# Weight splits of the SSD groups scheduled at the highest priority on ScalarE and VectorE

## The chip, the cores and the metric

The kernel runs on one core of a Trainium2 chip. The engines are TensorE (PE, matmuls and transposes), VectorE (DVE), ScalarE (ACT), GpSimd (POOL) and SyncE (SP), which mostly issues DMAs; each takes its own list of instructions and waits on semaphores where it needs another's result. The metric is the device time of one execution in microseconds (us).

## The reference, cut to what matters

A trunk of two layers for 512 tokens of width 1024, all in float32. Layer 0 mixes the tokens by a short gated convolution, layer 1 by a Mamba-2 SSD mixer with 8 groups; a SwiGLU network follows each. The change is in the SSD mixer:

```python
z, xbc, dt_raw = jnp.split(h @ w_in, [M_D_INNER, M_D_INNER + M_CONV_DIM], axis=-1)
xbc = jax.nn.silu(causal_depthwise_conv(xbc, conv_w) + conv_b)
xs, bm, cm = jnp.split(xbc, [M_D_INNER, M_D_INNER + g * n], axis=-1)
...
cb = jnp.einsum('bclgn,bcsgn->bclsg', cm, bm)
y_diag = jnp.einsum('bclsgr,bcsgrp->bclgrp', cb[..., None] * decay, xdt)
states = jnp.einsum('bclgn,bclgr,bclgrp->bcgrpn', bm, decay_to_end, xdt)
...
y_off = jnp.einsum('bclgn,bcgrpn,bclgr->bclgrp', cm, prev, jnp.exp(cs).astype(dtype))
...
y = y.reshape(bsz, s, M_D_INNER) * jax.nn.silu(z)
y = rms_normalize(y.reshape(bsz, s, g, M_D_INNER // g)).reshape(bsz, s, M_D_INNER) * norm_g
return y @ w_out
```

Each group has 256 columns of x, 128 of B, 128 of C and 256 of z.

## The kernel before, in words

Every float32 product is computed as three matmuls. A factor is split into a high half, rounded to the format that TensorE takes, and a low half, the rest: ACT casts the high half (L202) and DVE subtracts it from the source to get the low one (L203). The three matmuls per slice of 128 rows are high by high (L259), high by low (L260) and low by high (L261); the third is the first to need the weights' low half.

Weights come in by `load_w`: one DMA of 1 MB into a staging tile (`wst`, 2 buffers), then per 128 columns one split into a tile `whl` (4 buffers). Such a tile is the weight of one chunk: 8 slices by 3 matmuls, 24 matmuls of 512 columns into one PSUM tile `ip`. With 4 buffers the cast of a tile has to wait until PE has finished the chunk whose tile had the buffer before it, four tiles back.

A group takes six chunks: two of x (wx), B and C (wbc), two of z (wz). A pass of the loop over the groups (g = 1 to 7) finishes group g and projects group g + 1 beside it. PE's order in a pass is written by hand and fixed: wx0, `step_a` (transposes xtok and btokp, then cb), wx1, the states (`st`), wbc0, wbc1, `step_cc` (yo and yd, twice), z0, z1, and `step_d` (ssg, the norm's sum over the group). ssg needs accg, the sum of two squares of the gated output; cb needs ct and a free PSUM tile; the last matmuls of the states (L1053, st2) need the second half of xw.

The lists of ACT and DVE within the passes are made by a scheduler from priorities, which by default follow the order of the code, and from its own estimates of when operands are ready. On DVE stand, besides the splits, three taps of a convolution per chunk (cu, L957), xw and xdt from the transposed x (L1023, L1025), the mask of cb (L1037), the decay matrix csb (subtractions L1067, then a product L1074), the gated output (L1097 to L1107) and the norm (L1117, L1120). Instructions are taken in the order of the list. csb is filled by a DMA that ACT's queue issues (L944). Groups 0 and 1 lie in a stretch whose ACT and DVE order is written by hand too, with the splits passed through `later`.

Of the kernel before, what the change touches and what calls it, by code (L numbers as in the profile page):

```python
# [19 lines left out]
KD = D // P  # L20
DFF = 2816
NF = DFF // P
DIN = 2048
# [12 lines left out]
def trunk_kernel(  # L36
# [164 lines left out]
    def split_w(src, dst, nk):  # L201
        act.copy(dst[:, 0, :nk, :], src)  # L202
        dve.tensor_tensor(dst[:, 1, :nk, :], src, dst[:, 0, :nk, :].bitcast(F32), SUB)  # L203

    def load_w(srcs, nk=KD, k0=0, later=None):


        st = wst_p.tile([P, 8, 256], F32, tag="wst", name="wst")
        o = 0
        for m, c0, n in srcs:  # L210
            dma(st[:, :nk, o:o + n], m[k0 * P:(k0 + nk) * P, c0:c0 + n].rearrange("(k p) f -> p k f", p=P))
            o += n
        res = []
        for b in range(o // P):
            w = whl_p.tile([P, 2, 8, P], F32R, tag="whl", name="whl")
            sw = st[:, :nk, b * P:(b + 1) * P]
            if later is None:
                split_w(sw, w, nk)
            else:
                later.append((lambda sw=sw, w=w: act.copy(w[:, 0, :nk, :], sw),  # L220
                              lambda sw=sw, w=w: dve.tensor_tensor(w[:, 1, :nk, :], sw,
                                                                   w[:, 0, :nk, :].bitcast(F32), SUB)))
            res.append(w)
        return res
# [317 lines left out]
    wm_in, wm_out = m_w_in[0], m_w_out[0]  # L542

    with ExitStack() as ph:
# [96 lines left out]
        with tc.manual_schedule(engines={PE_ENGINE, mybir.EngineType.SP, mybir.EngineType.Activation,  # L641
# [122 lines left out]
            for name in OPENING.split():  # L764
                step(name)
            later = []
            next_cv = [load_w([(w_in0, (i + 1) * D + 2 * P, 256)], later=later) for i in range(2)]
            for hi, lo in later:
                hi()
# [20 lines left out]
        for jp in range(0, KD, 2):  # L790
            if jp == 0:
                pss = lead_ps[:4]
            else:
                ws = next_cv[0] + next_cv[1] if jp == 2 else [
                    w for i in range(2) for w in load_w([(w_in0, (i + 1) * D + jp * P, 256)])]
                pss = [in_chunk(w, h) for w in ws]
            us = [conv_mix_cv(jp + b, pss[b], pss[2 + b]) for b in range(2)]
            wb = load_w([(w_in0, jp * P, 256)]) if jp else None
            for b in range(2):
                a = act_tile(f"bu{jp + b}")  # L800
                conv_mix_b(us[b], in_chunk(wb[b], h) if jp else lead_ps[4 + b], a)
                acts.append(a)
            ada_next(2 if jp < 6 else 0)
            if jp == 4:
                put_gates(0)
                gg = make_gg(0, gg_tile)
                other_vectors(actp.tile([P, 8, P], F32, tag="a", name="rows2"))
# [57 lines left out]
    with ExitStack() as ph:  # L865
# [99 lines left out]
        class Group:  # L965
# [8 lines left out]
            def weights(self, i, later=None):  # L974
                g = self.g
                if i == 0:
                    self.wx = load_w([(wm_in, DIN + g * 256, 256)], later=later)
                elif i == 1:
                    self.wbc = load_w([(wm_in, 2 * DIN + g * P, P), (wm_in, 2 * DIN + D + g * P, P)],
                                      later=later)  # L980
                else:
                    self.wz = load_w([(wm_in, g * 256, 256)], later=later)

            def conv(self, i, pst):
                g = self.g
# [161 lines left out]
        with tc.manual_schedule(engines={PE_ENGINE, mybir.EngineType.Activation, mybir.EngineType.DVE}):  # L1147
            cur, nxt = Group(0), Group(1)
            later = []
# [365 lines left out]
```

## Time and profile before

| | |
|---|---|
| median of 3 runs | 1379.19 us (1378.7 to 1380.71) |
| profiled execution, its own time | 1379.55 us |
| its span, first to last instruction | 1377.5 us |
| PE busy | 1353.7 us, 98% |
| DVE busy | 911.7 us, 66% |
| ACT busy | 580.6 us, 42% |
| mean granted TensorE clock | 0.995 |

The passes 1 to 7 lie between some 669 and 960 us of the span; a steady pass takes 41 us. In a timeline row a number in brackets is the time for which the engine was idle ahead of the instruction, with what ended it. Matmuls are pipelined: rows of 0.39 us follow each other every 0.23 us, and a matmul that starts 0.63 us long and every 0.43 us ran at the lower granted clock.

### The profile page before, as it was taken

Reading aid. Unit: us, or ns where it says so; the run is one execution under the profiler, and the core shown is the slowest. Engines: PE = TensorE matmul, PEld = TensorE weight load, DVE = VectorE, ACT = ScalarE, POOL = GpSimd, SP = SyncE. Lnnn points to the kernel's source line nnn. Section 1 sums busy time; section 2 is a strip of 40 time slices with the busy share of each in tenths; the row PEclk is TensorE's granted clock in tenths of the full one; section 3 lists DMA queues with packets and bytes.
Section 4 is the critical chain, followed back from the end, with each engine's and each line's share of the span. In section 5 each row is a group of like instructions: output and inputs, shape, how many; then the busy total and the mean of one; then the engine's idle time right before and its main releaser. Section 6 shows DMA issues by size and latency. Waiting matters only on the chain.

```text
span 1377.5 us, 17633 instructions
## 1 busy us (share of the span) xinstructions
PE 1353.7 (98%) x6973; PEld 1135.5 (82%) x6973; DVE 911.7 (66%) x1485; ACT 580.6 (42%) x875; POOL 1.5 (0%) x11
## 2 busy tenths in 40 slices
PE   8999999999999999999899999999999999999997
PEld 7788889888888888898778888888889888887886
DVE  5777757478775222669878888777675655334867
ACT  5432247222222211665665656543473222223754
POOL 0000000000000000000000000000000000000000
PEclk9999999999999999999999999999999999999999
DMA  9956670468683322514344234332233987323743
GB/s 313 318 181 218 228 236 24 137 215 273 215 282 106 130 95 69 149 33 146 118 138 130 83 94 138 108 107 96 89 123 125 331 289 266 118 70 130 251 161 115
DMA packets 163702, 222.09 MB, mean 161 GB/s; under 512 B 7060, under 2 KB 112164, under 8 KB 161188
## 3 DMA queue, kind: packets, MB, share of 16 engines
q1 hardware_dynamic: 159616, 208.20, 45.9%
q10 hardware_dynamic: 4004, 12.77, 2.9%
q8 instruction: 55, 0.90, 0.3%
q14 instruction: 27, 0.22, 0.1%
HBM read 207.17 MB, written 13.78 MB: 160 GB/s over the span
## 4 chain that ended last, share of the span: by engine, by line
PE 64%; DVE 2%; DMA 1%; ACT 0%; issue 0%; SPq 0%; DVEq 0%; ACTq 0%
PE ip L259 11%; PE ip L261 11%; PE ip L260 11%; PE y L359 5%; PE y L361 5%; PE y L360 5%; PE li L259 2%; PE li L261 2%; PE li L260 2%; PE yd L1092 1%; PE yo L1086 1%; PE pa L1387 1%; PE pa L1388 1%; PE pz L1388 1%; PE pb L1388 1%; PE pz L1386 1%
## 5 line engine op out<-in xcount | busy, mean ns | idle before, releaser
L259 PE MATMUL ip<-h,whl 128*128 128x512 f32 x1096 | 434.2, 396 | 2.5 <-DVE cv L777 2.5
L261 PE MATMUL ip<-h,whl 128*128 128x512 f32 x1096 | 428.9, 391 | 6.6 <-DVE whl L203 6.6
L260 PE MATMUL ip<-h,whl 128*128 128x512 f32 x1096 | 427.8, 390 | 0.0
L261 PEld LDWEIGHTS ip<-h,whl 128*128 128x128 f32 x1096 | 206.4, 188 | 50.8 <-DVE whl L203 7.0
L259 PEld LDWEIGHTS ip<-h,whl 128*128 128x128 f32 x1096 | 206.7, 189 | 47.1 <-issue 5.2
L260 PEld LDWEIGHTS ip<-h,whl 128*128 128x128 f32 x1096 | 206.7, 189 | 43.2 <-issue 1.2
L202 ACT CAST whl<-wst 128x1024 fp32r<-128x1024 f32 (+1 forms) x163 | 152.2, 952 | 205.2 <-PE ip L261 161.0
L203 DVE TENSOR_TENSOR whl<-wst,whl 128x1024 fp32r<-128x1024 f32 (+1 forms) x163 | 176.9, 1101 | 61.8 <-ACT whl L202 61.1
L203 DVE TENSOR_TENSOR whlo<-wsto,whlo 128x1024 fp32r<-128x1024 f32 x46 | 56.3, 1223 | 96.6 <-ACT whlo L202 96.6
L126 DVE SCALAR_TENSOR_TENSOR ada_acc<-ada_st,csil,ada_acc 128x512 f32<-128x512 f32 x140 | 104.7, 749 | 22.8 <-DMA ada_st<-in_ada_w_dram 20.1
L202 ACT CAST whlo<-wsto 128x1024 fp32r<-128x1024 f32 x46 | 48.3, 1050 | 113.6 <-PE y L361 87.7
L259 PE MATMUL li<-h,whl 128*128 128x256 f32 x288 | 83.2, 289 | 0.0
L261 PE MATMUL li<-h,whl 128*128 128x256 f32 x288 | 81.6, 283 | 0.0
L260 PE MATMUL li<-h,whl 128*128 128x256 f32 x288 | 81.5, 283 | 0.0
L957 DVE SCALAR_TENSOR_TENSOR cu<-ip,cols,cu 128x511 f32<-128x511 f32 (+2 forms) x84 | 62.0, 741 | 13.7 <-ACT cu L954 13.5
L359 PE MATMUL y<-whlo,ff 128*128 128x512 f32 x176 | 68.6, 390 | 0.0
L361 PE MATMUL y<-whlo,ff 128*128 128x512 f32 x176 | 68.5, 389 | 0.0
L360 PE MATMUL y<-whlo,ff 128*128 128x512 f32 x176 | 68.5, 389 | 0.0
L259 PEld LDWEIGHTS li<-h,whl 128*128 128x128 f32 x288 | 55.3, 192 | 0.0
L260 PEld LDWEIGHTS li<-h,whl 128*128 128x128 f32 x288 | 55.2, 192 | 0.0
L261 PEld LDWEIGHTS li<-h,whl 128*128 128x128 f32 x288 | 55.1, 191 | 0.0
L359 PE MATMUL y<-whlo,ys 128*128 128x512 f32 x128 | 51.1, 399 | 0.0
(281 smaller groups left out, 1926.5 us busy)
## 6 DMA issues: line engine op xcount, KB each, us to landing
ada_st<-in_ada_w_dram SPq DMA_DIRECT2D x96, 512.0 KB, 5.8
wst<-in_f_w_in_dram SPq DMA_DIRECT2D x44, 1024.0 KB, 6.5
wst<-in_m_w_in_dram SPq DMA_DIRECT2D x14, 1024.0 KB, 5.7
tb<-in_f_w_out_dram SPq DMA_DIRECT2D x22, 512.0 KB, 7.4
td<-tb SPq DMA_DIRECT2D x11, 1024.0 KB, 4.9
wsto<-in_f_w_out_dram SPq DMA_DIRECT2D x10, 1024.0 KB, 4.8
wst<-in_m_w_in_dram SPq DMA_DIRECT2D x20, 512.0 KB, 5.2
wst<-in_a_w_in_dram SPq DMA_DIRECT2D x9, 1024.0 KB, 6.0
```

Source lines behind the costliest of these rows:

```text
L126: dve.scalar_tensor_tensor(acc, w, csil[:, k:k + 1], acc, MUL, ADD)
L202: act.copy(dst[:, 0, :nk, :], src)
L203: dve.tensor_tensor(dst[:, 1, :nk, :], src, dst[:, 0, :nk, :].bitcast(F32), SUB)
L259: pe.matmul(dst, w_at(w, 0, kk), a[:, 0, sl], start=start, stop=False)
L260: pe.matmul(dst, w_at(w, 0, kk), a[:, 1, sl], start=False, stop=False)
L261: pe.matmul(dst, w_at(w, 1, kk), a[:, 0, sl], start=False, stop=stop)
L359: pe.matmul(pst, a[:, 0, tk], wt[:, 0, kk, :], start=k == 0, stop=False)
L360: pe.matmul(pst, a[:, 0, tk], wt[:, 1, kk, :], start=False, stop=False)
L361: pe.matmul(pst, a[:, 1, tk], wt[:, 0, kk, :], start=False, stop=k == K - 1)
L957: dve.scalar_tensor_tensor(u[:, sft:], pst[:, :T - sft], w[3 - sft], u[:, sft:], MUL, ADD)
L1086: pe.matmul(pyo[:, sl], self.prev[:, cc - 1, q * P:(q + 1) * P], self.ct[:, sl], start=True, stop=True)
L1388: pe.matmul(acc[t], a[:, 1, sl], w[0], start=False, stop=True, skip_group_check=True)
```

## The change

`load_w` gets an argument `soon`. Where it is set, and no list `later` is given, the split's two instructions are put down under the scheduler's highest priority. The three loads of a group set it, so it acts on the splits of groups 2 to 7, and on nothing else.

```diff
-    def load_w(srcs, nk=KD, k0=0, later=None):
+    def load_w(srcs, nk=KD, k0=0, later=None, soon=False):
...
             if later is None:
-                split_w(sw, w, nk)
+                with tc.high_priority() if soon else ExitStack():
+                    split_w(sw, w, nk)
...
-                    self.wx = load_w([(wm_in, DIN + g * 256, 256)], later=later)
+                    self.wx = load_w([(wm_in, DIN + g * 256, 256)], later=later, soon=True)
...
-                                      later=later)
+                                      later=later, soon=True)
...
-                    self.wz = load_w([(wm_in, g * 256, 256)], later=later)
+                    self.wz = load_w([(wm_in, g * 256, 256)], later=later, soon=True)
```

No instruction's work changes. SP's list and POOL's are the same; on PE only the ssg of group 0 moves, from within the wx0 chunk of group 2 to its end; ACT loses two table loads and keeps all else, in another order; DVE keeps all, in another order. Lines of the new kernel past L218 are one higher.

DVE, end of pass 1's state update, before: the last cu taps of the wx1 chunk, the states' sums (prev), and behind them the splits of group 2's wbc tiles (whl_5662, whl_5665) and of its z tiles (whl_5777, whl_5780).

```order
L1056 TENSOR_TENSOR prev_5628<-prev_5628,dec_4979 128x256
L957 SCALAR_TENSOR_TENSOR cu_5622<-ip_5597,cols3_91,cu_5622 128x509
L1058 TENSOR_TENSOR prev_5628<-prev_5628,st01_5629 128x256
L1074 TENSOR_TENSOR csb_5401<-csb_5401,cbm_5590 128x1024
L1056 TENSOR_TENSOR prev_5628<-prev_5628,dec_4979 128x256
L203 TENSOR_TENSOR whl_5662<-wst_5659,whl_5662 128x1024
L1058 TENSOR_TENSOR prev_5628<-prev_5628,st2_5632 128x256
L203 TENSOR_TENSOR whl_5665<-wst_5659,whl_5665 128x1024
L203 TENSOR_TENSOR whl_5777<-wst_5775,whl_5777 128x1024
L203 TENSOR_TENSOR whl_5780<-wst_5775,whl_5780 128x1024
```

DVE in the new order, where the same two wbc splits stand now: within the gated output of group 0 (yg1) and the csb subtractions for group 2, ahead of accg and of all of pass 1's step_a.

```order
L1098 TENSOR_TENSOR y1_5441<-yo_5427,ecsb_5166 128x384
L203 TENSOR_TENSOR whl_5662<-wst_5659,whl_5662 128x1024
L1099 SCALAR_TENSOR_TENSOR yg1_5440<-xs1_4983,dcol_94,yd_5431 128x512
L1068 TENSOR_SCALAR csb_5524<-csb_5524,cs_tok_4977 128x128
L1100 TENSOR_TENSOR yg1_5440<-yg1_5440,y1_5441 128x384
L1068 TENSOR_SCALAR csb_5524<-csb_5524,cs_tok_4977 128x128
L1101 TENSOR_TENSOR yg1_5440<-yg1_5440,zs1_5207 128x512
L1068 TENSOR_SCALAR csb_5524<-csb_5524,cs_tok_4977 128x128
L203 TENSOR_TENSOR whl_5665<-wst_5659,whl_5665 128x1024
```

Both have moved up past the whole of step_a, the first states and the products of csb.

DVE at step_a of pass 1, before: the two halves of xw and xdt stand together.

```order
L1023 TENSOR_TENSOR xw_5569<-xtok_5570,dte_tok_4978 128x512
L1025 TENSOR_TENSOR xdt_5568<-xtok_5570,dt_tok_4976 128x512
L1023 TENSOR_TENSOR xw_5569<-xtok_5577,dte_tok_4978 128x256
L1025 TENSOR_TENSOR xdt_5568<-xtok_5577,dt_tok_4976 128x512
L1037 TENSOR_TENSOR cbm_5590<-cb_5591,mask_82 128x512
```

The same place in the new order, with a tap of cu and the split of group 2's first z tile in it:

```order
L1024 TENSOR_TENSOR xw_5569<-xtok_5570,dte_tok_4978 128x512
L958 SCALAR_TENSOR_TENSOR cu_5449<-ip_5373,cols3_91,cu_5449 128x509
L203 TENSOR_TENSOR whl_5777<-wst_5775,whl_5777 128x1024
L1026 TENSOR_TENSOR xdt_5568<-xtok_5570,dt_tok_4976 128x512
L1024 TENSOR_TENSOR xw_5569<-xtok_5577,dte_tok_4978 128x256
L1026 TENSOR_TENSOR xdt_5568<-xtok_5577,dt_tok_4976 128x512
```

The split and the tap have come between the first xw and the first xdt, whose source xtok holds the PSUM buffer that cb takes next.

DVE at step_a of pass 4, before: xw and xdt of group 4, then the mask and a wbc split of group 5; the split of group 5's second z tile (whl_6746) comes 13 rows below these.

```order
L1023 TENSOR_TENSOR xw_6535<-xtok_6536,dte_tok_4978 128x512
L957 SCALAR_TENSOR_TENSOR cu_6528<-ip_6503,cols3_91,cu_6528 128x509
L1025 TENSOR_TENSOR xdt_6534<-xtok_6536,dt_tok_4976 128x512
L1023 TENSOR_TENSOR xw_6535<-xtok_6543,dte_tok_4978 128x256
L1025 TENSOR_TENSOR xdt_6534<-xtok_6543,dt_tok_4976 128x512
L1037 TENSOR_TENSOR cbm_6556<-cb_6557,mask_82 128x512
L203 TENSOR_TENSOR whl_6631<-wst_6625,whl_6631 128x1024
```

The same place in the new order:

```order
L1024 TENSOR_TENSOR xw_6535<-xtok_6536,dte_tok_4978 128x512
L958 SCALAR_TENSOR_TENSOR cu_6528<-ip_6503,cols3_91,cu_6528 128x510
L1026 TENSOR_TENSOR xdt_6534<-xtok_6536,dt_tok_4976 128x512
L203 TENSOR_TENSOR whl_6746<-wst_6741,whl_6746 128x1024
L958 SCALAR_TENSOR_TENSOR cu_6528<-ip_6503,cols3_91,cu_6528 128x509
L1024 TENSOR_TENSOR xw_6535<-xtok_6543,dte_tok_4978 128x256
L1026 TENSOR_TENSOR xdt_6534<-xtok_6543,dt_tok_4976 128x512
L1038 TENSOR_TENSOR cbm_6556<-cb_6557,mask_82 128x512
```

whl_6746 now stands between the two halves of xw (xw_6535 from xtok_6536 and from xtok_6543). Its cast takes the buffer of the wx1 chunk's weights. In the other passes the split of the second z tile stands behind the second half of xw.

Likewise on DVE ahead of the ssg of pass 1: the split of group 3's first wbc tile (whl_5984) stood behind accg's sum of group 1, and now stands ahead of that sum and of the gated output's second half (y1, its sum and product); its cast takes the buffer of the first z chunk of that pass.

## Rows read from the trace of the kernel before

**Rows 1.** Page, busy time by engine (share of the span).

```profile
PE 1353.7 (98%) x6973; PEld 1135.5 (82%) x6973; DVE 911.7 (66%) x1485; ACT 580.6 (42%) x875; POOL 1.5 (0%) x11
```

**Rows 2.** What PE waited for, 640 to 1000 us: total, times, longest.

```profile
PE ip L261 <- DVE whl L203: 6.6, 1, 6.6
PE cb L1036 <- DVE xdt L1025: 0.7, 1, 0.7
```

**Rows 3.** Windows: us; PE, PEld, DVE, ACT, POOL busy (count); clock; DMA share; GB/s.

```profile
688.00:689.00 1.00, 0.00 (x0) 0.00 (x0) 1.00 (x3) 1.00 (x1) 0.00 (x0) 0.87 0.00 0
689.00:695.00 6.00, 2.83 (x7) 2.25 (x8) 6.00 (x9) 4.75 (x7) 0.00 (x0) 0.50 0.04 5
64.50:67.50 3.00, 3.00 (x7) 2.36 (x8) 3.00 (x7) 1.67 (x3) 0.00 (x0) 0.50 1.10 363
720.00:920.00 200.00, 200.00 (x1061) 165.94 (x1060) 168.37 (x271) 115.32 (x140) 0.00 (x0) 1.00 0.35 108
```

**Rows 4.** PE timeline, pass 1: start, length, instruction, [idle before <-what ended it].

```profile
677.23 1.13 PE L1036 MATMUL cb<-ct,bt 128*128 128x128 f32 x8 [0.71 <-DVE xdt L1025]
...
685.19 0.39 PE L260 MATMUL ip<-h,whl 128*128 128x512 f32 x1
692.17 0.79 PE L261 MATMUL ip<-h,whl 128*128 128x512 f32 x1 [6.60 <-DVE whl L203]
...
695.68 0.39 PE L260 MATMUL ip<-h,whl 128*128 128x512 f32 x1
```

**Rows 5.** ACT timeline, pass 1, casts of group 2's wbc tiles.

```profile
679.32 1.98 ACT L202 CAST whl<-wst 128x1024 fp32r<-128x1024 f32 x2
```

**Rows 6.** DVE timeline, pass 1.

```profile
675.80 0.69 DVE L1023 TENSOR_TENSOR xw<-xtok,dte_tok 128x512 f32<-128x512 f32 x1 [3.47 <-PE xtok L1019]
676.40 0.68 DVE L1025 TENSOR_TENSOR xdt<-xtok,dt_tok 128x512 f32<-128x512 f32 x1
...
690.90 1.22 DVE L203 TENSOR_TENSOR whl<-wst,whl 128x1024 fp32r<-128x1024 f32 x1
```

**Rows 7.** PE timeline, pass 4, end of wx1 and the states.

```profile
813.61 0.39 PE L261 MATMUL ip<-h,whl 128*128 128x512 f32 x1
...
814.29 0.39 PE L261 MATMUL ip<-h,whl 128*128 128x512 f32 x1
...
815.38 0.59 PE L1053 MATMUL st<-xw,btok 128*128 128x256 f32 x2
```

**Rows 8.** ACT timeline, pass 4, cast of the second z tile.

```profile
815.85 1.05 ACT L202 CAST whl<-wst 128x1024 fp32r<-128x1024 f32 x1
```

**Rows 9.** DVE timeline, pass 4.

```profile
812.59 0.41 DVE L1023 TENSOR_TENSOR xw<-xtok,dte_tok 128x256 f32<-128x256 f32 x1
...
815.53 0.75 DVE L957 SCALAR_TENSOR_TENSOR cu<-ip,cols,cu 128x511 f32<-128x511 f32 x1 [0.20 <-ACT cu L954]
```

**Rows 10.** DVE and PE timeline, pass 1, output of the group and ssg.

```profile
711.40 0.55 DVE L1097 TENSOR_TENSOR y<-yo,ecsb 128x384 f32<-128x384 f32 x1
...
712.81 0.28 DVE L1067 TENSOR_SCALAR csb<-csb,cs_tok 128x128 f32<-128x128 f32 x1 [0.27 <-DMA csb<-cs_d]
713.01 0.68 DVE L1100 TENSOR_TENSOR yg<-yg,zs 128x512 f32<-128x512 f32 x1
...
718.99 1.02 PE L1114 MATMUL ssg<-accg,ones 128*128 128x512 f32 x2
```

**Rows 11.** ACT's queue and DVE, pass 3; DVE and PE, pass 4.

```profile
789.70 0.33 ACTq L944 DMA_DIRECT2D csb<-cs_d  x1
...
795.33 0.29 DVE L1067 TENSOR_SCALAR csb<-csb,cs_tok 128x128 f32<-128x128 f32 x1 [0.91 <-DMA csb<-cs_d]
...
838.72 0.68 DVE L1107 TENSOR_TENSOR accg<-accg,sqg 128x512 f32<-128x512 f32 x1
...
841.40 1.02 PE L1114 MATMUL ssg<-accg,ones 128*128 128x512 f32 x2
```

**Rows 12.** PE timeline, layer 0, the end of an idle time.

```profile
64.40 0.77 PE L259 MATMUL ip<-h,whl 128*128 128x512 f32 x1 [2.55 <-DVE cv L777]
```

## The prediction

> **What bounds the kernel now.** I read the page's busy times first: PE is busy 98% of the span, DVE 66%, ACT 42% [rows 1]. So only what makes PE wait, or its clock fall, can cost or give time. Next I read the waits of PE over the passes in question (640 to 1000 us). There are two: once a matmul of L261 waits 6.6 us for a weight split on DVE (L203), once cb waits 0.7 us for an xdt [rows 2]. Both fall in pass 1. In the steady passes PE is busy for 200.00 of 200 us while DVE has 168 and ACT 115 [rows 3]: no wait is left there to take away, and every wait the new order makes there is new.
>
> Last I read the timelines around the long wait, engine by engine, to see what is behind what. On PE the second matmul of the wbc chunk starts at 685.19, the third only at 692.17 [rows 4]. ACT had cast both hi halves from 679.32 to 681.30 [rows 5]; DVE took up the first lo half at 690.90 [rows 6], 9.6 us after that cast. So the split was late by its place on DVE, not by its data. The Trainium skill ("PSUM — Partial Sum Buffer", Engine vs sequencer instructions) calls the queues of ScalarE and VectorE strict FIFO; the row agrees for this split, and by the same rule a split that is raised before its data are there holds up all behind it, which is what the added terms below are.
>
> **What goes.** In the new order the two wbc splits of group 2 stand among the group's first csb subtractions, long before their chunk. Their casts wait for the slots that the two z chunks before free. The second of these ends at about 669 (cb's 677.23 [rows 4] less 0.7 of waiting, 2 of transposes, 5.44 for the wx0 chunk of 24 matmuls and 0.45 for ssg); with a cast of 1.0 and a split of 1.2 us [rows 5, 6] both are done some 14 us before 685.2, and the wait goes whole. A steady matmul comes every 0.227 us (813.61 to 814.29 holds three [rows 7]). The third matmul was due at 685.19 + 0.23 = 685.42 and came at 692.17: 6.75. The clock had fallen meanwhile: 0.87 in 688 to 689, 0.50 (1.2 GHz) from 689 to 695 [rows 3]; the eight intervals from 692.17 to 695.68 [rows 4] took 3.51 in place of 8 x 0.227 = 1.81: 1.70 more. Together **-8.45 us**. What is late next there is nothing within 5 us.
>
> In passes 2 to 7 the edit gives nothing: four slots hold the split weights, so a cast can only begin when PE has finished the chunk four tiles back, and before it did so already (pass 4: the wx1 chunk's last matmul begins at 814.29, the cast into its slot at 815.85 [rows 7, 8], and its own chunk, z1's, is the fourth from there). The wait is hidden behind 5.4 us of matmuls per chunk. ACT has two table loads fewer; it is 42% busy and none of its table loads is waited for, so nothing.
>
> **What is added, first: cb in pass 1.** The new order puts a cu and the split of z's first tile between the first xw and the first xdt. xw starts at 675.80 and xdt 0.60 later now [rows 6]; after, the cu (0.75 [rows 9]) and the split (1.22 [rows 6]) come first, 1.97 at their lengths, about 1.8 since one instruction starts 0.08 ahead of the former's end (675.80 + 0.69 against 676.40). The split's own cast can begin when the wx0 chunk ends, four transposes (some 0.5) ahead of the xw, so it is done by 676.4, before its turn at 677.05, and adds nothing. cb already waits for that xdt (677.23 [rows 4]), so all of it shows: **+1.8** (ends 0 and 2.0), and PE's idle time there becomes 0.71 + 1.8 = 2.5 us.
>
> **Second: ssg of pass 1.** It is due when z1's chunk ends: 718.99 now [rows 10], 718.99 - 8.45 + 1.8 = 712.34 after. In the new order the split of group 3's first wbc tile stands ahead of y1, its add, its product and accg. Its cast waits for z0's chunk, 5.44 us before (707.0 with the last matmul's tail): cast to 708.1, split to 709.25, then y1, a csb subtraction (0.20, from 712.81 to 713.01), the add, another subtraction and the product: 711.40 to 713.69 now with one subtraction and 0.27 of waiting in it [rows 10], so 2.0 plus the overlap, to 711.3; five subtractions 1.0, with ACT's square beside them; accg 0.68 [rows 11] to 713.0. **+0.6** (ends 0 and +2, by whether the csb transfer has landed by then).
>
> **Third: st2 in pass 4.** Here alone z1's split stands ahead of the second xw; in the other passes it follows it. That split's cast waits for the last matmul of the wx1 chunk, and st2, five matmuls on, waits for that xw. A ring: PE's own chunk, cast, split, cu, xw, PE. From the start of the last matmul (814.29): its 0.39, cast 1.05 [rows 8], split 1.14 to 1.22, cu 0.66 to 0.75 [rows 9], xw 0.41 [rows 9], and 0.2 for the hand-overs between engines (of it 0.15 from DVE to PE: the first xdt ends at 676.40 + 0.68, cb begins at 677.23 [rows 4, 6]): 3.85 to 4.0, where st2 is due after 815.38 - 814.29 = 1.09 [rows 7]. **+2.75** (ends 2.5 and 3.1). Now the xw is done at 813.0, before that point.
>
> In the other passes the ssg has least to spare. Now accg's add ends at 839.4 and ssg starts at 841.40 [rows 11]. After, from the landing of csb: 0.2 + 0.5 + 0.2 + 0.6, seven subtractions 1.4, split 1.14, accg 0.68: 4.7 us, and ssg is due 10.9 after the transfer's issue (830.5, one chunk pair before 841.40). A landing takes 795.33 - 789.70 = 5.6 at most now [rows 11], so at least 0.6 us are left; I take nothing (ends 0 and 1 us for each of five passes).
>
> **The clock.** PE idles 2.5 us at the first place and 2.7 at the third. The nearest row: an idle time of 2.55 us ahead of 64.40 [rows 12], after which the clock stood at 0.50 from 64.5 to 67.5 [rows 3], 1.5 us lost over those 3 us at half pace. In the long wait the fall came about 3.2 us after 685.6. So one fall has been seen by 2.55 us and one only after 3.2: I give each place an even chance and **+1.7** for one fall (that of row 692.17), none or two as ends. The Trainium skill ("TensorE: Matmul & The Clock Gate", What's actually happening) says that the watch on activity runs free, so that the same gap can lower the clock in one run and not in the next; by it the three runs of the result may differ by 1.7 us, and the sum would be the same.
>
> **Sum.** -8.45 + 1.8 + 0.6 + 2.75 = -3.3, and with one fall -1.6. The profiled execution took 1379.55 (span 1377.5 and 2.05 around it), 0.36 above the median of the runs shown, 1379.19. From the median: 1375.9 with no fall, **1377.5** with one, 1379.2 with two.
>
> **Rivals.**
> Only the long wait goes (0.10): the two places where a split overtakes what PE waits for don't bite, because DVE reaches them earlier than I count. 1379.2 - 8.45 + at most 2 = 1370.7 to 1372.7. For it: in 200 us of steady passes PE never waited. Against: both places follow from the order alone, and the third is a ring with PE in it.
> No net change (0.13): both clock falls come, or the second wait is at its upper end: 1379 to 1380.5. For it, row 64.40.
> Slower (0.17): ssg is late in every pass. Place: csb's seven subtractions and the split of the next wbc tile, both ahead of accg. It decides when csb lands more than 6.2 us after its issue; splits done sooner free the staging tiles sooner, and the 1 MB weight transfers then start nearer to csb's. Price: 1 us per us beyond 6.2 in each of passes 2 to 6. At a landing of 7.5 us 1.3 x 5 = 6.5: 1377.5 + 6.5 = 1384, over 1382 from 7.1 us on. For it: csb's landing is waited for today (0.91 us of DVE at 795.33). Against: 0.6 to 1.5 us to spare as it lands now.
> The change doesn't do what it says (0.02): the split still comes late; 1379.
>
> **Chances and range.** My forecast with no or one fall has 0.58 (0.20 and 0.38), the rivals 0.10, 0.13, 0.17 and 0.02. 0.2% is 2.8 us, about what a measurement of this kernel tells from no change: below 1376.4 is faster, above 1382 slower. Faster: 0.10 + 0.17 of the case without a fall (its 1375.9 is just under the line) + 0.09 of the one-fall case, 0.36; slower 0.17; the same 0.47. The range from 1373 to 1382.5 leaves out most of the first rival and most of the slower one, 0.2 in all; the likeliest case's own range is 1375.5 to 1379.5.
>
> **What would show it.** In the new profile: no wait of L261 for L203 in the wbc chunk of pass 1; cb of pass 1 waiting about 2.5 us for xdt; the st2 of pass 4 waiting about 2.7 us for xw, with the cast just behind the chunk's last matmul; ssg of pass 1 waiting under 1 us for accg; granted clock 0.50 for some 3 us behind one of the first two. Wrong would be: any wait of PE in passes 2, 3, 5, 6 or 7; ssg waiting in pass after pass; or neither cb nor st2 waiting longer than before.

## The result, and the profile after

The changed kernel took 1388.08 us (median of 6 runs, 1384.65 to 1390.26), the kernel before 1379.88 beside it (6 runs, 1377.73 to 1381.77): ratio 1.0057, interval 1.0046 to 1.0068. It is slower by 8 us where 1.7 less was forecast. The profiled execution of it took 1384.74 us, span 1382.7, so its trace shows 5.2 of the 8 us.

The page's busy times, the answer to [rows 1], show none of it: PE is at 98% again.

```profile
PE 1355.5 (98%) x6973; PEld 1136.2 (82%) x6973; DVE 912.4 (66%) x1485; ACT 576.8 (42%) x873; POOL 1.5 (0%) x11
```

The waits of PE from 640 to 1000 us in the changed kernel (in total, times, longest), the answer to [rows 2]:

```profile
PE ssg L1115 <- DVE accg L1108: 6.4, 5, 2.3
PE st L1054 <- DVE xw L1024: 2.5, 1, 2.5
PE cb L1037 <- DVE xdt L1026: 2.5, 1, 2.5
```

The 6.6 us wait for a weight split is gone. The cb and st2 waits of the forecast are there, and ssg waits in five passes for accg. The PE timeline of the changed kernel has each of them (start, length, instruction, idle time before it):

```profile
677.23 1.45 PE L1037 MATMUL cb<-ct,bt 128*128 128x128 f32 x8 [2.50 <-DVE xdt L1026]
...
685.27 1.02 PE L1052 MATMUL st<-xw,btok 128*128 128x256 f32 x4
...
713.98 1.10 PE L1115 MATMUL ssg<-accg,ones 128*128 128x512 f32 x2 [1.67 <-DVE accg L1108]
...
756.20 1.10 PE L1115 MATMUL ssg<-accg,ones 128*128 128x512 f32 x2 [1.18 <-DVE accg L1108]
...
799.57 1.10 PE L1115 MATMUL ssg<-accg,ones 128*128 128x512 f32 x2 [2.33 <-DVE accg L1108]
...
818.70 0.70 PE L1054 MATMUL st<-xw,btok 128*128 128x256 f32 x2 [2.52 <-DVE xw L1024]
...
846.00 1.10 PE L1115 MATMUL ssg<-accg,ones 128*128 128x512 f32 x2 [0.99 <-DVE accg L1108]
...
887.29 1.10 PE L1115 MATMUL ssg<-accg,ones 128*128 128x512 f32 x2 [0.28 <-DVE accg L1108]
...
928.17 1.02 PE L1115 MATMUL ssg<-accg,ones 128*128 128x512 f32 x2
```

Against the starts before (cb 677.23 and ssg 718.99 and 841.40 in [rows 4, 10, 11]; the states of pass 1 at 683.66 and the other ssg at 759.79, 800.60, 882.21 and 923.02 in the same trace), the distance of the two kernels runs like this:

| place | after minus before, us | what lies between |
|---|---|---|
| transposes of pass 1 | -1.80 | layer 0: an idle time of 2.14, not 2.55, and no lower clock behind it |
| cb, pass 1 | 0.00 | cb waits 2.50, not 0.71 |
| states, pass 1 | +1.61 | lower clock behind that wait |
| ssg, pass 1 | -5.01 | -8.45 of the long wait, +1.67 |
| ssg, pass 2 | -3.59 | +1.18 |
| ssg, pass 3 | -1.03 | +2.33 |
| ssg, pass 4 | +4.60 | lower clock behind the wait of pass 3 (about 1.6), st2 2.52, ssg 0.99 |
| ssg, pass 5 | +5.08 | +0.28 |
| ssg, pass 6 | +5.15 | nothing |

Each ssg wait cost about 0.2 us more than its length: 1.42, 2.56 and 0.48 us from pass to pass in 2, 3 and 5, where the waits are 1.18, 2.33 and 0.28. Most of the 1.80 us of the first line (1.6) is there before 69 us of the span, in layer 0, which the change does not touch; from the transposes on, the changed kernel lost 5.15 + 1.80 = 6.95 us.

The clock, in the windows of the changed kernel (us, then busy time and count of PE, PEld, DVE, ACT, POOL, then the granted clock):

```profile
678.00:681.00 3.00, 3.00 (x10) 2.46 (x9) 2.48 (x6) 2.97 (x5) 0.00 (x0) 0.50 0.00 0
802.00:804.00 2.00, 2.00 (x6) 1.63 (x5) 0.03 (x1) 1.96 (x4) 0.00 (x0) 0.50 0.31 56
820.00:823.00 3.00, 3.00 (x15) 2.46 (x14) 3.00 (x7) 0.75 (x2) 0.00 (x0) 1.00 1.03 276
```

It was down to 0.50 (1.2 GHz) behind cb's 2.50 us of idle time, and again behind ssg's 2.33 in pass 3, and it stayed at 1.00 behind st2's 2.52.

Why ssg is late is read in pass 3, across the queues (SPq and ACTq rows are the issue of a transfer); the first row is the split of the next group's second x tile:

```profile
783.88 1.22 DVE L203 TENSOR_TENSOR whl<-wst,whl 128x1024 fp32r<-128x1024 f32 x1
...
785.12 0.37 SPq L211 DMA_DIRECT2D wst<-in_m_w_in_dram  x1
...
786.19 0.33 ACTq L945 DMA_DIRECT2D csb<-cs_d  x1
...
794.77 0.29 DVE L1068 TENSOR_SCALAR csb<-csb,cs_tok 128x128 f32<-128x128 f32 x1 [4.39 <-DMA csb<-cs_d]
...
797.61 1.21 DVE L203 TENSOR_TENSOR whl<-wst,whl 128x1024 fp32r<-128x1024 f32 x1
798.75 0.68 DVE L1108 TENSOR_TENSOR accg<-accg,sqg 128x512 f32<-128x512 f32 x1
```

z's weights (1 MB) are issued at 785.12, csb at 786.19, and DVE gets the first csb element at 794.77: 8.6 us after its issue, where it was 5.6 before [rows 11]. z's transfer is issued as soon as the x split is done (783.88 + 1.22 = 785.10), whose staging tile it takes. Before, that split (the second of the two in the first row here) was done only at 793.96, and the transfer was issued over four us behind csb's:

```profile
791.61 2.35 DVE L203 TENSOR_TENSOR whl<-wst,whl 128x1024 fp32r<-128x1024 f32 x2
...
793.98 0.37 SPq L211 DMA_DIRECT2D wst<-in_m_w_in_dram  x1
```

In the changed kernel, from the landing to the end of accg there are 794.77 to 799.43, 4.7 us, among them the wbc split of 797.61.

### The profile page after: what moved, and what is told of

Its sections match the earlier page's. It is cut to its first block, busy times and chain, and to the rows that moved or that the text cites. A ratio compares the mean times of both kernels' runs of the same rounds, so it can differ in the third digit from the quotient of the medians.

```text
span 1382.7 us, 17664 instructions
## 1 busy us (share of the span) xinstructions
PE 1355.5 (98%) x6973; PEld 1136.2 (82%) x6973; DVE 912.4 (66%) x1485; ACT 576.8 (42%) x873; POOL 1.5 (0%) x11
## 4 chain that ended last, share of the span: by engine, by line
PE 60%; DVE 3%; DMA 3%; ACT 1%; issue 0%; DVEq 0%; ACTq 0%
PE ip L260 10%; PE ip L261 10%; PE ip L262 10%; PE y L360 5%; PE y L361 5%; PE y L362 5%; DMA csb<-cs_d 3%; PE li L260 2%; PE li L262 2%; PE li L261 2%; PE yd L1093 1%; PE yo L1087 1%; PE pa L1388 1%; PE pb L1388 1%; PE pb L1387 1%; PE pa L1389 1%
```

## The experiments

All are edits of the changed kernel; the times stand beside runs of the kernel before on the same chip.

**Hold back one transfer.** The lists of PE, ACT, DVE and SP are those of the changed kernel; GpSimd, otherwise idle, makes z's transfer wait for csb's landing.

```diff
+        if hold is not None:
+            nc.gpsimd.tensor_copy(st[:1, 0, :1], hold[:1, 0, :1])
...
-                    self.wz = load_w([(wm_in, g * 256, 256)], later=later, soon=True)
+                    self.wz = load_w([(wm_in, g * 256, 256)], later=later, soon=True, hold=self.e if g > 2 else None)
```

> The changed kernel with every list unchanged, but GpSimd copies one element of the freshly landed csb tile into the staging tile ahead of the transfer of z's weights (groups 3 to 7), so that this 1 MB transfer starts behind csb's landing and not about 1.2 us ahead of its issue. Theory A (the two transfers run side by side; csb then lands 6.5 to 9.6 us after its issue, and ssg waits): csb lands about 5.5 us after issue again, the ssg waits fall from 6.4 us in five passes to under 1 us in all, cb (2.5 us) and st2 of pass 4 (2.5 us) stay; time = before - 8.45 + 1.8 + 2.5 + 0 to 1 + 0 to 3.4 of clock = 1376 to 1380 us. Theory B (the split ahead of accg, whose cast waits for z0's chunk, makes ssg late by itself, the transfers don't matter): ssg waits stay at 6 us or so, 1386 to 1388 us. Theory C (another transfer than z's delays csb): csb lands as late as in the changed kernel, same time as that.

Measured: 1378.29 us, ratio 0.9986 (0.9977 to 0.9995), 10 us under the changed kernel. Its waits of PE, and pass 3 across the queues:

```profile
PE st L1054 <- DVE xw L1024: 2.5, 1, 2.5
PE cb L1037 <- DVE xdt L1026: 2.5, 1, 2.5
PE ssg L1115 <- DVE accg L1108: 0.6, 1, 0.6
```

```profile
790.89 0.37 SPq L211 DMA_DIRECT2D wst<-in_m_w_in_dram  x1
...
785.91 0.33 ACTq L945 DMA_DIRECT2D csb<-cs_d  x1
...
790.90 0.29 DVE L1068 TENSOR_SCALAR csb<-csb,cs_tok 128x128 f32<-128x128 f32 x1 [0.80 <-POOL wst L208]
...
793.75 1.22 DVE L203 TENSOR_TENSOR whl<-wst,whl 128x1024 fp32r<-128x1024 f32 x1
794.88 0.69 DVE L1108 TENSOR_TENSOR accg<-accg,sqg 128x512 f32<-128x512 f32 x1
...
796.81 1.02 PE L1115 MATMUL ssg<-accg,ones 128*128 128x512 f32 x2
```

csb is used 5.0 us after its issue (its transfer took 4.6 in the list of DMA issues; from issue to first use the changed kernel took 6.5 to 8.6 over passes 1 to 5, and the kernel before 4.6 to 5.6). accg is done at 795.6, and ssg starts at 796.81 without a wait, though the split stands ahead of accg as it did. Only pass 1's ssg waits, 0.57. Theory A holds; B and C fall.

**wbc alone.**

```diff
-                    self.wx = load_w([(wm_in, DIN + g * 256, 256)], later=later, soon=True)
+                    self.wx = load_w([(wm_in, DIN + g * 256, 256)], later=later)
...
-                    self.wz = load_w([(wm_in, g * 256, 256)], later=later, soon=True)
+                    self.wz = load_w([(wm_in, g * 256, 256)], later=later)
```

> High priority for the wbc splits alone. The splits of group 2's wbc tiles are early (the long wait goes), the first wbc split of each next group stands ahead of accg, and the wx splits stay where they were, so z's transfer starts behind csb's. Theory A (ssg is late only by csb's late landing together with the split ahead of accg): csb lands in 5.5 us, no ssg wait, no st2 wait; 1379.9 - 8.4 = 1371 to 1373 us. Theory B (the split ahead of accg is enough): about 1 us of ssg wait in each of passes 2 to 6, 1376 to 1378 us.

Measured: 1370.86 us, ratio 0.9927 (0.9915 to 0.9940). The only wait of PE left in the passes:

```profile
PE cb L1037 <- DVE xdt L1026: 0.7, 1, 0.7
```

csb lands in 4.8 us (pass 3), and the split ahead of accg costs nothing by itself, so B falls here too.

**wx alone.**

```diff
-                                      later=later, soon=True)
+                                      later=later)
...
-                    self.wz = load_w([(wm_in, g * 256, 256)], later=later, soon=True)
+                    self.wz = load_w([(wm_in, g * 256, 256)], later=later)
```

> High priority for the wx splits alone. The 6.6 us wait for group 2's wbc split stays. The second wx split stands earlier, so z's transfer starts near csb's issue; no wbc split ahead of accg except in pass 4. Theory A: csb lands in 7 to 9 us; accg is ready about 3.6 us after landing without the split, so ssg waits 0 to 1.5 us in a pass, most in pass 4 where the split is ahead of it (2 us or more); 1381 to 1385 us. Theory B: no ssg wait but in pass 4; 1379 to 1381 us.

Measured: 1383.71 us, ratio 1.0020 (1.0011 to 1.0029).

```profile
PE ip L262 <- DVE whl L203: 6.5, 1, 6.5
PE ssg L1115 <- DVE accg L1108: 2.8, 2, 1.5
```

The long wait is back, and ssg waits 1.27 in pass 2 and 1.54 in pass 3. The one pass with the split ahead of accg is pass 3 in the list, not 4 as I had counted, and its wait is the longer one, by less than I expected. The transfer beside csb is in passes 3 to 5 another one than I had said, the pair of half-megabyte transfers of the wbc weights, but as near (here pass 3); in pass 2 that pair is issued 2.3 us ahead of csb and z's transfer 0.9 us ahead.

```profile
791.24 0.99 SPq L211 DMA_DIRECT2D wst<-in_m_w_in_dram  x2
...
792.50 0.33 ACTq L945 DMA_DIRECT2D csb<-cs_d  x1
```

So an early weight transfer makes csb late in each of these passes (first used 6.8 to 8.4 us after its issue, passes 1 to 5), and whether ssg waits goes by what DVE still has to do then. In passes 4 and 5 DVE took 3.1 us from csb's first use to the end of accg, with no split in it, and ssg did not wait, with csb used at 7.1 and 7.4; the changed kernel, with the split, took 4.2 there and waited, with csb used at 7.7 and 7.0. In pass 2 the order put other work behind csb (the product y and more of its subtractions), 4.2 us too, and ssg waited without a split.

**All but wx.**

```diff
-                    self.wx = load_w([(wm_in, DIN + g * 256, 256)], later=later, soon=True)
+                    self.wx = load_w([(wm_in, DIN + g * 256, 256)], later=later)
```

> High priority for the wbc and z splits, not for wx. The long wait goes; z's transfer starts behind csb's as before; the wbc split stands ahead of accg in all passes; the second z split stands ahead of the second xw in passes 2 and 5. Theory A: csb lands in 5.5 us, no ssg wait; st2 waits 2.5 us in passes 2 and 5; cb 0.7 us; 1379.9 - 8.4 + 5 + 0 to 3.4 of clock = 1376.5 to 1380 us. Theory B: 6 us of ssg waits beside it, 1382 us or more.

Measured: 1378.17 us, ratio 0.9983 (0.9974 to 0.9992).

```profile
PE st L1054 <- DVE xw L1024: 4.4, 2, 2.5
PE cb L1037 <- DVE xdt L1026: 0.7, 1, 0.7
```

As theory A has it: no ssg wait, csb in 4.8 us (pass 3), and two st2 waits, 1.86 and 2.52, from the second z split ahead of the second xw (in passes 2 and 4; I had counted 5 for the second). The granted clock fell behind both, behind the shorter one too (the matmul that had waited starts at 727.22):

```profile
728.00:731.00 3.00, 3.00 (x8) 2.34 (x7) 3.00 (x7) 0.46 (x1) 0.00 (x0) 0.50 1.02 279
```

**All but z.**

```diff
-                    self.wz = load_w([(wm_in, g * 256, 256)], later=later, soon=True)
+                    self.wz = load_w([(wm_in, g * 256, 256)], later=later)
```

> High priority for the wx and wbc splits, not for z. The long wait goes; cb of pass 1 waits 0.7 us as before and no z split stands ahead of an xw, so st2 doesn't wait; the second wx split is early, so z's transfer starts about 1 us ahead of csb's issue, and the wbc split stands between csb's landing and accg. Theory A: csb lands in 7 to 9 us, ssg waits 1 to 2.5 us in four or five passes, 5 to 9 us in all; 1380 - 8.4 + 5 to 9 + clock = 1377 to 1383 us, that is 6 to 12 us above wbc_only, from which it differs by the wx priority alone. Theory B (the split ahead of accg is enough) has fallen with wbc_only; under a theory D (what the wx splits cost in the changed kernel is DVE's and ACT's time ahead of the gated output, not the transfer) csb would land in 5 us and ssg wait as long.

Measured: 1383.09 us, ratio 1.0014 (1.0004 to 1.0024), at the upper edge of A's range and 12 us above wbc_only, from which it differs by the wx priority alone. The execution in the trace, 1379.61, was the fastest of the twelve, so the trace shows 8 of these 12.

```profile
PE ssg L1115 <- DVE accg L1108: 5.4, 4, 2.1
PE cb L1037 <- ACT ct L960: 1.4, 1, 1.4
PE st L1054 <- DVE xw L1024: 0.5, 3, 0.2
```

```profile
779.66 0.99 SPq L211 DMA_DIRECT2D wst<-in_m_w_in_dram  x2
...
782.82 0.37 SPq L211 DMA_DIRECT2D wst<-in_m_w_in_dram  x1
...
784.07 0.33 ACTq L945 DMA_DIRECT2D csb<-cs_d  x1
```

ssg waits 0.58 to 2.08 in four passes; csb is first used 7.4 to 8.5 us after its issue in these. Here both the wbc pair and z's transfer are issued in the 4.4 us ahead of csb's. Theory D falls.

**z alone.**

```diff
-                    self.wx = load_w([(wm_in, DIN + g * 256, 256)], later=later, soon=True)
+                    self.wx = load_w([(wm_in, DIN + g * 256, 256)], later=later)
...
-                                      later=later, soon=True)
+                                      later=later)
```

> High priority for the z splits alone. Group 2's wbc splits are still late and now have its z splits ahead of them: the long wait stays at 6.6 us or grows by up to 2.3. z's second split stands ahead of the second xw of pass 3: st2 waits 2.5 us there. csb lands in 5.5 us, no ssg wait. Before + 2.5 to 5 + 0 to 1.7 of clock = 1382 to 1387 us. If z's priority costs nothing by itself: 1380 us.

Measured: 1391.38 us, ratio 1.0080 (1.0067 to 1.0093), above what was expected.

```profile
PE ip L262 <- DVE whl L203: 11.8, 2, 8.8
PE st L1054 <- DVE xw L1024: 1.9, 1, 1.9
```

```profile
686.59 2.36 DVE L203 TENSOR_TENSOR whl<-wst,whl 128x1024 fp32r<-128x1024 f32 x2
...
694.28 1.22 DVE L203 TENSOR_TENSOR whl<-wst,whl 128x1024 fp32r<-128x1024 f32 x1
```

The two z splits (2.36 us at 686.59) now stand ahead of the wbc split of 694.28, and the long wait grew from 6.60 to 8.85, as counted. I had missed a second one: in pass 5 the order put a wbc split behind the products of csb, and PE waits 2.98 us for it at 873.30. The clock fell behind that wait and behind st2's 1.86.

**wbc of group 2 alone.** No priority at wx and z, and at wbc:

```diff
-                                      later=later, soon=True)
+                                      later=later, soon=g == 2)
```

> High priority for the two wbc splits of group 2 alone, all other groups as before. If the whole gain of the change is the one long wait, this equals wbc_only: 1370 to 1372 us, and the priority in groups 3 to 7 gives and costs nothing there. If early splits in the steady passes gave something, it would be slower than wbc_only by that.

Measured: 1371.06 us, ratio 0.9931 (0.9920 to 0.9943): the same as wbc_only. The whole gain is one wait in pass 1. Both beat the kernel before by 0.7% and the changed kernel by some 17 us.

**The changed kernel again.**

> The changed kernel once more, for a second profile: the first profiled execution (1384.7 us) was 3.4 us under the median of its runs (1388.1). Theory A: the same waits at the same places (cb 2.5, st2 of pass 4 2.5, ssg in passes 1 to 5), the ssg waits 6 to 10 us in all by how the two transfers meet, and the lower clock behind none to four of these places at 1.5 us each; 1384 to 1390 us. If something outside the SSD passes makes up the difference, the waits there are 6.4 us again and the time is lost elsewhere.

Measured: 1388.89 us (4 runs), ratio 1.0063 (1.0040 to 1.0087); the profiled execution took 1387.68. The ssg waits are 7.1 us in all (2.37, 1.43, 2.61, 0.26, 0.42), cb and st2 2.5 each as before. The clock fell at other places:

```profile
677.00:681.00 4.00, 1.50 (x13) 1.25 (x12) 3.81 (x8) 2.96 (x5) 0.00 (x0) 1.00 0.25 68
713.00:720.00 7.00, 4.63 (x12) 2.97 (x11) 4.63 (x13) 4.65 (x6) 0.00 (x0) 0.76 0.47 137
803.00:808.00 5.00, 4.65 (x19) 3.57 (x20) 2.80 (x9) 4.94 (x6) 0.00 (x0) 1.00 0.15 32
820.00:826.00 6.00, 5.14 (x16) 4.10 (x17) 6.00 (x11) 2.55 (x3) 0.00 (x0) 0.72 0.69 178
```

Behind cb (2.50 at 679.80) it stayed at 1.00, behind ssg of pass 1 (2.37 at 715.65) it fell, behind ssg of pass 3 (2.61 at 803.35) it did not, and behind st2 (2.52 at 820.86) it did. It fell in layer 0 too, behind an idle time of 2.6 us there. The ssg waits are 0.7 us longer than in the first trace, within the first expectation's 6 to 10, but most of the difference lies outside the passes, as the second one had it: this execution is 2.9 us longer (1387.68 against 1384.74), and cb of pass 1 starts 2.57 us later already (679.80 against 677.23). The first trace was the lucky one: of the ten here it alone has no fall of the clock in layer 0. The profiled executions of the changed kernel are both below its median, so what the slowest runs lose beyond this stays open; more of these falls at once would do it, and was not seen.

## Why the prediction was wrong

Right were four steps, three of them in size too. The long wait goes: -8.45 forecast, and wbc2_only, which does that alone, gained 9.5 us (7.9 to 11.0, by its ratio); in its trace cb and ssg of pass 1 lie 8.42 us nearer to each other than before (677.61 and 710.95, against 677.23 and 718.99). The 2 us counted there for the transposes of pass 1 are 1.4 in the trace before (675.16 to 676.52), which moves nothing, since the splits are done long before they are needed. cb in pass 1: +1.8 forecast, 2.50 - 0.71 = 1.79 measured. st2 in pass 4: +2.75 forecast, 2.52 measured, with the ring as it was drawn:

```profile
815.35 1.04 ACT L202 CAST whl<-wst 128x1024 fp32r<-128x1024 f32 x1 [3.10 <-PE ip L262]
...
816.43 1.23 DVE L203 TENSOR_TENSOR whl<-wst,whl 128x1024 fp32r<-128x1024 f32 x1 [2.50 <-ACT whl L202]
817.57 0.74 DVE L958 SCALAR_TENSOR_TENSOR cu<-ip,cols,cu 128x509 f32<-128x509 f32 x1
818.23 0.41 DVE L1024 TENSOR_TENSOR xw<-xtok,dte_tok 128x256 f32<-128x256 f32 x1
```

The cast begins 0.04 behind the end of the chunk, then split, cu and xw, and st2 at 818.70. ssg of pass 1: +0.6 forecast, 1.67 measured in the changed kernel, and 0.57 where z's transfer was held back; the upper end of +2 was given for a late csb, and that was it. An even chance for a fall of the clock at an idle time of 2.5 us was about right: in the trace of the changed kernel, its second one, and the one with z held back, nine idle times of 2.33 to 2.61 us in the passes lowered it five times (behind cb in hold_z: 0.76 over 677 to 684; st2 there: 1.00). A shorter one did it too: 1.86 us ahead of st2 lowered it in no_wx and in wz_only, while 2.08 us ahead of ssg in no_wz did not. The Trainium skill ("TensorE: Matmul & The Clock Gate", What's actually happening) calls the watch on activity free-running, and these rows are in line with that: the same 2.50 us ahead of the same cb did it in one execution and not in the other.

The step that failed is the one that says of the ssg in the other passes "I take nothing". It took csb's landing from the trace before ("5.6 at most now") and so left out what the change does to transfers. Measured there: 1.18 + 2.33 + 0.99 + 0.28 = 4.78 us, another 1.1 in pass 1, about 0.2 more per wait, and a second fall of the clock, behind ssg's wait in pass 3 (about 1.6 us), where the sum had one. The rest of the sum stands: hold_z, which takes these waits away but for 0.57 in pass 1, measured 0.14% under the kernel before, 1.9 us, where the sum with one fall has 1.6. The rival named as slower was what happened, in its place and for its reason, and I gave it 0.17. Its price was near: with landings of 7.9, 8.6, 7.7 and 7.0 us in passes 2 to 5 the rule "1 us per us beyond 6.2" gives 1.7, 2.4, 1.5 and 0.8, against 1.18, 2.33, 0.99 and 0.28, so the point from which it decides is 6.7 in passes 2, 4 and 5, and 6.25 in pass 3.

Its chance could have been worked out. The transfer of z's weights waits for the staging buffer that the second wx split gives back. Before, that split stood behind the gated output's first half, and in pass 3 the transfer went out at 793.98, over 4 us behind csb's. In the new order it stands ahead of it, as soon as the wbc1 chunk has ended. From there step_cc's 3.7 us of matmuls (704.30 to 707.97 in the trace before) run to csb's issue; the tail of the last matmul (0.2), a cast of 1.05, a split of 1.2 and hand-overs of 0.1 leave the transfer 1.1 us ahead of csb's, and it was issued 1.07 ahead. That csb would then land late was in the rival, and the runs showed by how much. For the sum I followed each raised split to who waits for its data and for its place in the list; who waits for the buffer that it gives back stands only in the rival, and there no time of issue was worked out.

The argument that the steady passes had no wait to lose held for what could be gained (wbc2_only equals wbc_only). It did not hold for what could be lost: PE was busy for 200 of 200 us there because accg was 2 us early [rows 11], and the change used up these 2 us twice, once by the split ahead of accg (1.2) and once by csb (1 to 3). The split alone costs no ssg wait (wbc_only, no_wx, and hold_z past pass 1). The early transfer without the wbc priority (wx_only) costs 2.8 us in all, of which 1.54 fell in the one pass that has the split as well; with both it is 6.4 and 7.1.

## What to carry to other kernels

When an instruction that frees a buffer moves up, follow the buffer: write down which transfer it releases, when that goes out now, and what other transfer it will meet. A stage whose bound engine never waits can be near its edge; list the slack of every operand that it takes, and add up all that a change takes from the same one. Raise the priority of the one load that is late, not of its whole class: here two splits out of 36 carried all of the gain, and the rest cost 17 us.

## What the runs showed of the hardware that was not expected

A 1 MB broadcast transfer (csb) took 4.6 us where no weight transfer ran beside it (hold_z, pass 3). In the kernel before it took 4.6 to 5.6 from issue to first use, with a weight transfer issued 3.3 to 4.9 us behind it, and in four of the five passes a pair of half a megabyte each over 4 us ahead. With a weight transfer of 1 MB issued 1.1 to 1.3 us ahead of it on another queue it took 6.5 to 8.6. In pass 3 of the changed kernel the transfer that started first did not finish first and leave the other its full rate: the weights took 9.8 us, where 5.3 is the median of the 1 MB weight transfers over the passes, and the two ended within 0.2 us of each other, so both were slowed. The granted clock fell or not behind idle times of TensorE of equal length, 2.50 us in both executions of the changed kernel, and it fell behind one of 1.86 us in no_wx.
